# The gated input of a streaming encoder layer, computed with tokens on partitions and turned by VectorE

## The chip, the cores and the metric

The kernel runs on one core of a Trainium2 chip. The metric is the device time of one execution in microseconds (us). The kernel before took 1996.45 us, the median of three runs (1996.19 to 1996.85).

## The reference

One layer of a streaming encoder is computed for 384 tokens: 256 of a new stream and 8 x 16 of running streams. D_MODEL is 2048, D_CONV is 1024, there are 8 heads of 128, and everything is float32. Cut to what matters:

```python
h = rmsnorm(x, norm_mix_g)
proj = h @ w_in            # columns: GLU in (2 x 1024) | q | k | v | forget | gate A | gate B
u = glu_in[..., :D_CONV] * jax.nn.sigmoid(glu_in[..., D_CONV:])
ext = jnp.concatenate([conv_buf, u], axis=1)          # 30 older rows ahead
z = layernorm(causal_dwconv(ext, conv_dw_w, conv_dw_b), conv_ln_g, conv_ln_b)   # 31 taps
a_out = (z * jax.nn.sigmoid(z)) @ conv_pw_out
new_conv = ext[:, -(CONV_W - 1):]                     # an output
b_out = attn_fn(q, k, v, logf) @ w_att_out            # 8 heads, logits + cumsum of log f
x = x + (gate_a * a_out + gate_b * b_out) @ w_out
x = x + (silu(dwconv3(g_half)) * u_half) @ w_down     # up-projected from rmsnorm(x)
```

## The kernel before

Every product runs on TensorE as three matmuls: both operands are split into a high and a low part, and high x high, high x low and low x high are added in PSUM. The loop `gemm` (L227) does a list of jobs, a job being one strip of 512 weight columns over 16 k-steps (8 in some). Two k-steps make a unit: one weight tile `raw` of 128 x 2 x 512 is fetched by SyncE's DMA queue (L139), ScalarE copies its high part (`hi`, L148), VectorE subtracts to get the low part (`lo`, L149). `ahead(3)` asks for up to three units in advance, and `raw`, `hi` and `lo` have three buffers each, so no split can be more than three units ahead of TensorE. PSUM is divided into five `acc` buffers for jobs and three `misc` buffers, most of them for side work.

After each k-step `tick` runs side work: items put off with `after`, then one step of the attention generator, then one step of the convolution generator. TensorE follows the source. On VectorE, ScalarE and SyncE a scheduler sets the order from dependencies and priorities: a split is moved up by SPLIT_AHEAD, attention by ATT_AHEAD, an evacuation of PSUM by EVAC_AHEAD. `queued` chains an instruction behind the last queued one on its engine.

The stages are: the V, Q and K projections; the GLU stage (4 jobs, 64 k-steps) with attention and the start of the convolution as side work; the gates GA and GB (8 jobs) with the rest of the convolution and then its LayerNorm as side work; the output projections; the feed-forward part.

In the GLU stage head h stands at k-step 5 + 6h plus an offset: `head_operands` at +1 (VectorE turns the cached keys, `kTs`, L611, and pads the queries, `qz`), `head_scores` at +4 (TensorE L622 to L630 into three `misc` buffers, VectorE L636 to L640, ScalarE L639 and L641), `head_probs` at +9 (TensorE transposes into two `misc` buffers, which ScalarE's `pT`, L650, and VectorE's `pz`, L653, empty), `head_out` at +12 (`on`, `attT`), `head_last` at +14 (`attT`, L676). Head h+1's scores so stand one k-step behind head h's probabilities.

The weights of GLU job g are 256 columns of each half. The job is of kind "A": the weights are stationary and the result has features on partitions, four blocks of 128 x 384. Evacuation (L702) is four VectorE multiplications by `rs1b` (the norm's factor, spread over partitions by L336 to L344), two sigmoids and two products on GpSimd, into `ut`, features on partitions. All other jobs are of kind "B": tokens on partitions, three blocks of 128 x 512.

The convolution handles the 8 blocks of 128 channels one after another, 17 k-steps apart; block c's tap w (L752 for w = 0, L754 for the rest, 128 x 384 on VectorE) stands at step 17c + w, so in most k-steps two taps stand. Three steps ahead of a block's first tap `fill(c)` builds `ext`: a VectorE transpose of the old state (L731), three ScalarE copies (L733, L736, L737), and for the state that is handed out two TensorE transposes of `ut` (L740, L741), two ScalarE copies and two DMAs.

Of the kernel before, what the change touches and what calls it, by code (L numbers as in the profile page):

```python
# [29 lines left out]
CONV_FIRST, CONV_LAG = 24, 17  # L30
# [3 lines left out]
SPLIT_AHEAD, ATT_AHEAD, EVAC_AHEAD = 150, 250, 400  # L34
# [6 lines left out]
def hybrid_step(  # L41
# [36 lines left out]

    mm = nc.tensor.matmul
    tr = nc.tensor.transpose  # L80
    tt = nc.vector.tensor_tensor
    stt = nc.vector.scalar_tensor_tensor
    ts = nc.vector.tensor_scalar
# [28 lines left out]
    def newton_rsqrt(r, s, m):  # L112
        queued(nc.scalar.activation(s, m, AF.Sqrt), in_first())
        nc.vector.reciprocal(r, s)
        tt(s, r, r, op=ALU.mult)
        tt(s, s, m, op=ALU.mult)
        ts(s, s, -0.5, 1.5, op0=ALU.mult, op1=ALU.add)
        tt(r, r, s, op=ALU.mult)
# [27 lines left out]
    def split_rows(hi, lo, raw, o, k):  # L146
        first = in_first()
        queued(nc.scalar.copy(hi[:, k, :o], raw[:, k, :o]), first)  # L148
        queued(tt(lo[:, k, :o], raw[:, k, :o], f(hi[:, k, :o]), op=ALU.subtract), first)  # L149
# [77 lines left out]
    def gemm(jobs, sides=(), wide=False):  # L227
        for js in jobs:
            js = js if isinstance(js, tuple) else (js,)
            for j in js:  # L230
                nb = 4 if j["kind"] == "A" else NTT
                j["ps"] = [(misc_tile if i == 2 and (wide or j is not js[0]) else acc_tile)() for i in range(nb)]
            for j, k in [(j, k + i) for k in range(0, js[0]["nk"], 2) for j in js for i in range(2)]:
# [7 lines left out]
                for m in range(nb):  # L241
                    s = slice(m * P, (m + 1) * P)
                    if j["kind"] == "A":
                        o = ps[m][:, :NT]
                        mm(o, hi[:, kk, s], ah, start=st, stop=False)  # L245
                        mm(o, hi[:, kk, s], al, start=False, stop=False)  # L246
                        mm(o, lo[:, kk, s], ah, start=False, stop=sp)  # L247
                    else:
                        o = ps[m][:, :n]
                        mm(o, ah[:, s], hi[:, kk, :n], start=st, stop=False)  # L250
                        mm(o, ah[:, s], lo[:, kk, :n], start=False, stop=False)  # L251
                        mm(o, al[:, s], hi[:, kk, :n], start=False, stop=sp)  # L252
                if sp:
                    with tc.high_priority(offset=EVAC_AHEAD):
                        for m in range(nb):
                            j["evac"](m, ps[m])
                    if "post" in j:
# [5 lines left out]
    def blocks(rows, put):  # L263
        src = rows.rearrange("p t (m b j) -> p b m t j", m=4, b=4)
        for b in range(4):
            for a in range(4):
                nc.vector.transpose(put(a, slice(32 * b, 32 * b + 32)), src[32 * a:32 * a + 32, b])  # L267
# [8 lines left out]
    def job(kind, nk, act, evac, n=512, done=None):  # L276
        d = dict(kind=kind, nk=nk, act=act, evac=evac, n=n)
# [12 lines left out]
    def x_chunk(c):  # L290
# [5 lines left out]
        with tc.high_priority(offset=EVAC_AHEAD):  # L296
            queued(nc.scalar.activation(hi, ps[:, :NT], AF.Identity, scale=g))  # L297
# [4 lines left out]
    with tc.manual_schedule(engines={ENG.SP, ENG.Activation, ENG.DVE}):  # L302
        nc.vector.memset(junk[:, 0:1], 0.0)
        nc.scalar.dma_start(gm_row[:], norm_mix_g[0].rearrange("(c p) -> c p", p=P))
        nc.scalar.activation(junk[:, 1:2], junk[:, 0:1], AF.Identity)
# [16 lines left out]
        nc.vector.tensor_copy(gm[:], pv[:, :16])  # L322
# [10 lines left out]
    rs1b = cp.tile([P, NT], F32, name="rs1b")  # L333
# [6 lines left out]
    def over_partitions(dg, dst):  # L340
# [3 lines left out]
        nc.scalar.copy(dst, ps[:, :NT])  # L344
# [46 lines left out]
    def small_columns():  # L391
        ps = misc_tile()
        tr(ps[:, :R_N], vrow[:R_N, :], ident[:R_N, :R_N])
        nc.vector.tensor_copy(col[:], ps[:, :R_N])
        ts(qgs[:], col[:, R_QG:R_QG + 1], float(P) ** -0.5, None, op0=ALU.mult)

    def first_norm():
        for c in range(2, 16, 2):
# [6 lines left out]
            if c % 4 == 2:  # L405
                for t in range(NTT):
                    n = c // 4
                    sq = nc.scalar.activation(junk[:], xs[n][:, t, :], AF.Square, accum_out=ssx[:, t, n:n + 1])
# [9 lines left out]
        with tc.high_priority(offset=EVAC_AHEAD):  # L418
            nc.vector.tensor_reduce(mt[:], ssx[:], axis=mybir.AxisListType.X, op=ALU.add)
            ts(mt[:], mt[:], 1.0 / DM, EPS, op0=ALU.mult, op1=ALU.add)  # L420
            r = rsqrt(mt[:], [P, NTT], p_x0, "r1")
            nc.vector.tensor_copy(rs1[:], r[:])
# [3 lines left out]
        yield  # L426
        dg = diagonals(p_x0.tile([P, NTT, P], F32, name="r1d"), rs1)
        yield
        yield
        over_partitions(dg, rs1b[:])  # L430
# [6 lines left out]
    def tok_job(dst, c0, n, sq):  # L437
        d = job("B", 16, ha, tok_evac(dst, c0, n))

        def post():  # L440
            for t in range(NTT):
                for h in range(c0 // P, (c0 + n) // P):
                    jk = p_qkv.tile([P, P], F32, tag="jk", bufs=2, name="jk")
                    nc.scalar.activation(jk[:], dst[:, t, h * P:(h + 1) * P], AF.Square,
# [4 lines left out]
    def tok_evac(dst, c0, n, shared=True):  # L449
        def ev(t, ps):  # L450
            if shared and t % 2:
                ts(dst[:, t, c0:c0 + n], ps[:, :n], rs1[:, t:t + 1], None, op0=ALU.mult)
            else:
                queued(nc.scalar.activation(dst[:, t, c0:c0 + n], ps[:, :n], AF.Identity, scale=rs1[:, t:t + 1]),
# [4 lines left out]
    v_jobs = [job("B", 16, ha, tok_evac(vt, 344 * i, 344, shared=i == 2), n=344) for i in range(3)]  # L459
# [11 lines left out]
    nc.scalar.activation(e[:], e[:], AF.Exp, scale=-1.0)  # L471
    ts(r[:], e[:], 2.0, None, op0=ALU.add)
    nc.vector.reciprocal(r[:], r[:])
# [27 lines left out]
    def bias_rows():  # L501
        for _ in range(6):
            yield
        for i in range(2):
# [3 lines left out]
            nc.vector.tensor_copy(cw[:, i * 124:(i + 1) * 124], ps[:, :124])  # L508
            nc.vector.tensor_copy(fw[:, i * 66:(i + 1) * 66], ps[:, 128:128 + 66])
# [5 lines left out]
        nc.scalar.activation(crow[:, :2 * P], ps[:H, :2 * P], AF.Copy, scale=-1.0)  # L515
        ps = misc_tile()
        mm(ps[:H, :P], lg[:, 2, :], bm[:], start=True, stop=True)
        nc.scalar.activation(crow[:, 2 * P:], ps[:H, :P], AF.Copy, scale=-1.0)
# [3 lines left out]
        nc.scalar.copy(drow[:], ps[:64, :P])  # L522
# [18 lines left out]
    def q_panel(n):  # L541
        blocks(qt[:, :, 512 * n:512 * (n + 1)], by_feature(attT[:, 4 * n:4 * n + 4]))
        for h in range(4 * n, 4 * n + 4):
            nc.scalar.activation(attT[:, h], attT[:, h], AF.Identity, scale=qgs[:])
# [64 lines left out]
    def head_past_keys(d):  # L609
        kTs = p_att.tile([P, 8, P], F32, tag="kTs", bufs=1, name="kTs")  # L610
        nc.vector.transpose(kTs[:].rearrange("p b k -> p (b k)"), kcs[d["h"]][:])  # L611
        d["kTs"] = kTs

    def head_operands(d):
        head_past_keys(d)
        d["bs"] = bss[d["h"]]
        nc.vector.tensor_copy(qz[d["h"] % 2][:, :, :, 0:16], by_stream(attT[:, d["h"], 2 * P:]))
# [489 lines left out]
```

## Time and profile before

| what | before |
|---|---|
| median of 3 runs | 1996.45 us |
| the profiled execution | 1998.56 us |
| its span, first to last instruction | 1996.7 us |
| granted TensorE clock, mean | 0.999 |
| TensorE busy | 1986.5 us (99%) |
| VectorE busy | 1305.3 us (65%) |
| ScalarE busy | 743.2 us (37%) |
| VectorE busy in 214 to 386 us (GLU stage) | 142.22 of 172 us |
| VectorE busy in 386 to 600 us (gates) | 167.21 of 214 us |

The profiled execution lies 2.11 us over the median, 1.86 us of it outside the span. A matmul of 512 columns takes 0.39 us from start to end, but the next one starts 0.23 us after it, so the rate of TensorE is read from start to start, and so it is with VectorE: of a run of equal instructions the timeline gives start, length and count. "L754" is line 754 of the kernel before.

### The profile page before, as it was taken

To read this page: it belongs to the slowest core of one execution; us is meant where nothing else is said; L and a number is where in the kernel's file an instruction comes from. 1 tells how busy PE (TensorE), PEld (TensorE's weight loads), DVE (VectorE), ACT (ScalarE), POOL (GpSimd) and SP (SyncE) were. 2 spreads that over 40 slices of the span, in tenths; PEclk is the share of its full clock that TensorE was granted. 3 is DMA by queue.
4 is the path that set the end of the run, shared out by engine and by line. 5 is a ranking of instruction groups with operands and counts; after the bars stand their busy time and mean duration, and the time that the engine had idled before them with its cause. 6 is when DMAs were issued, how large, how long until landed. Compare 5 with 4: busy or idle time off the path is not lost.

```text
span 1996.7 us, 24449 instructions
## 1 busy us (share of the span) xinstructions
PE 1986.5 (99%) x9383; PEld 1676.0 (84%) x9383; DVE 1305.3 (65%) x1908; ACT 743.2 (37%) x1077; POOL 89.5 (4%) x216
## 2 busy tenths in 40 slices
PE   9999999999999999999999999999999999999999
PEld 9888999888888888888888888888888888888887
DVE  4455889788755487676867683377673376638663
ACT  5535354433334433344333432233332233323321
POOL 1000011100000000000000000010000000000000
PEclk9999999999999999999999999999999999999999
DMA  6564767444443334534344443444433444343443
GB/s 184 149 188 117 216 154 161 141 140 131 130 129 124 128 125 163 165 122 137 119 137 126 129 134 129 129 126 127 136 129 132 132 118 137 128 133 120 138 158 106
DMA packets 209254, 275.98 MB, mean 138 GB/s; under 512 B 55878, under 2 KB 96729, under 8 KB 209129
## 3 DMA queue, kind: packets, MB, share of 16 engines
q1 hardware_dynamic: 208817, 273.85, 46.0%
q8 instruction: 73, 1.20, 0.3%
q0 software_dynamic: 288, 0.57, 0.1%
q14 instruction: 44, 0.36, 0.1%
q10 hardware_dynamic: 32, 0.01, 0.0%
HBM read 266.98 MB, written 7.86 MB: 138 GB/s over the span
## 4 chain that ended last, share of the span: by engine, by line
PE 96%; DVE 2%; DMA 1%; issue 0%; SPq 0%; ACT 0%; DVEq 0%; ACTq 0%
PE acc L252 20%; PE acc L250 20%; PE acc L251 20%; PE misc L252 10%; PE misc L251 10%; PE misc L250 10%; PE acc L245 2%; PE acc L247 2%; PE acc L246 2%; DVE lo L149 1%; DMA raw<-in_w_in_dram 0%; DVE mixT L267 0%; DVE ut L754 0%; DMA vc<-in_cache_v_dram 0%; DMA bs<-c_dr 0%
## 5 line engine op out<-in xcount | busy, mean ns | idle before, releaser
L149 DVE TENSOR_TENSOR lo<-raw,hi 128x1024 fp32r<-128x1024 f32 (+2 forms) x481 | 580.5, 1207 | 530.7 <-ACT hi L148 526.8
L148 ACT CAST hi<-raw 128x1024 fp32r<-128x1024 f32 (+2 forms) x481 | 496.3, 1032 | 970.1 <-PE misc L252 841.1
L250 PE MATMUL acc<-hi,xg 128*128 128x512 f32 x704 | 274.9, 390 | 0.0
L252 PE MATMUL acc<-hi,xg 128*128 128x512 f32 x704 | 273.9, 389 | 0.0
L251 PE MATMUL acc<-lo,xg 128*128 128x512 f32 x704 | 273.9, 389 | 0.0
L250 PE MATMUL acc<-hi,hT 128*128 128x512 f32 (+1 forms) x512 | 193.0, 377 | 0.5 <-ACT hT L297 0.5
L252 PE MATMUL acc<-hi,hT 128*128 128x512 f32 (+1 forms) x512 | 190.4, 372 | 0.2
L251 PE MATMUL acc<-lo,hT 128*128 128x512 f32 (+1 forms) x512 | 190.3, 372 | 0.0
L250 PEld LDWEIGHTS acc<-hi,xg 128*128 128x128 f32 x704 | 132.1, 188 | 28.4
L754 DVE SCALAR_TENSOR_TENSOR ut<-ext,cw,ut 128x384 f32<-128x384 f32 x240 | 151.9, 633 | 6.0
L252 PEld LDWEIGHTS acc<-hi,xg 128*128 128x128 f32 x704 | 132.1, 188 | 27.5
L251 PEld LDWEIGHTS acc<-lo,xg 128*128 128x128 f32 x704 | 132.2, 188 | 27.1
L252 PE MATMUL misc<-hi,xg 128*128 128x512 f32 x352 | 137.0, 389 | 0.0
L250 PE MATMUL misc<-hi,xg 128*128 128x512 f32 x352 | 137.0, 389 | 0.0
L251 PE MATMUL misc<-lo,xg 128*128 128x512 f32 x352 | 136.9, 389 | 0.0
L250 PE MATMUL acc<-hi,act 128*128 128x512 f32 x352 | 136.9, 389 | 0.0
L251 PE MATMUL acc<-lo,act 128*128 128x512 f32 x352 | 136.9, 389 | 0.0
L252 PE MATMUL acc<-hi,act 128*128 128x512 f32 x352 | 136.9, 389 | 0.0
L267 DVE STREAM_TRANSPOSE extf<-tok 32x384 f32<-32x384 f32 x176 | 100.3, 570 | 30.9 <-ACT tok L988 28.2
L267 DVE STREAM_TRANSPOSE uT<-tok 32x384 f32<-32x384 f32 x176 | 100.3, 570 | 29.7 <-ACT tok L988 26.9
L250 PEld LDWEIGHTS acc<-hi,hT 128*128 128x128 f32 x512 | 96.2, 188 | 16.1 <-ACT hT L297 1.0
L252 PEld LDWEIGHTS acc<-hi,hT 128*128 128x128 f32 x512 | 96.1, 188 | 15.7 <-DVE hT L298 0.7
(325 smaller groups left out, 3133.8 us busy)
## 6 DMA issues: line engine op xcount, KB each, us to landing
raw<-in_w_up_dram SPq DMA_DIRECT2D x176, 512.0 KB
raw<-in_w_in_dram SPq DMA_DIRECT2D x96, 512.0 KB
raw<-in_w_down_dram SPq DMA_DIRECT2D x88, 512.0 KB
raw<-in_w_in_dram SPq DMA_DIRECT2D x64, 256.0 KB
raw<-in_w_out_dram SPq DMA_DIRECT2D x32, 512.0 KB
raw<-in_w_att_out_dram SPq DMA_DIRECT2D x16, 512.0 KB
raw<-in_conv_pw_out_dram SPq DMA_DIRECT2D x16, 512.0 KB
raw<-in_w_in_dram SPq DMA_DIRECT2D x23, 344.0 KB
```

The source lines that it names most:

```text
L148: queued(nc.scalar.copy(hi[:, k, :o], raw[:, k, :o]), first)
L149: queued(tt(lo[:, k, :o], raw[:, k, :o], f(hi[:, k, :o]), op=ALU.subtract), first)
L245: mm(o, hi[:, kk, s], ah, start=st, stop=False)
L246: mm(o, hi[:, kk, s], al, start=False, stop=False)
L247: mm(o, lo[:, kk, s], ah, start=False, stop=sp)
L250: mm(o, ah[:, s], hi[:, kk, :n], start=st, stop=False)
L251: mm(o, ah[:, s], lo[:, kk, :n], start=False, stop=False)
L252: mm(o, al[:, s], hi[:, kk, :n], start=False, stop=sp)
L267: nc.vector.transpose(put(a, slice(32 * b, 32 * b + 32)), src[32 * a:32 * a + 32, b])
L754: stt(o, v, wc, o, op0=ALU.mult, op1=ALU.add)
```

## The change

- The GLU jobs become kind "B", and the kind "A" goes. Block t of a job now holds 128 tokens; columns 0 to 255 are the gate, 256 to 511 the value.
- Evacuation per job: three ScalarE sigmoids (128 x 256, straight from PSUM) and three VectorE `scalar_tensor_tensor` (128 x 256, from PSUM) into `ur`, tokens on partitions. `glu_done` then puts sixteen VectorE transposes of 32 x 192 (`ut<-ur`) into the next four k-steps, four a step. `rs1b` and the six matmul passes that spread it go.
- `fill` loses its two TensorE transposes, two ScalarE copies and two DMAs; the state is handed out by two DMAs from `ur` after the last job.
- A wrapper, `InOrder`, chains every VectorE and ScalarE instruction through the GLU stage in source order, evacuations excepted, which are still moved up. ATT_AHEAD goes. After the stage the scheduler orders again by priority.
- The normalization of a head's probabilities moves to a step of its own (`head_scale`, at +5), with one reciprocal for three. The cached keys are loaded two heads ahead, and the loads of the side work get SPLIT_AHEAD. The convolution starts two k-steps later (CONV_FIRST 24 to 26).

The core of the diff (plain renamings to the wrapped engines and of `job` left out):

```diff
-CONV_FIRST, CONV_LAG = 24, 17
+CONV_FIRST, CONV_LAG = 26, 17
-SPLIT_AHEAD, ATT_AHEAD, EVAC_AHEAD = 150, 250, 400
+SPLIT_AHEAD, EVAC_AHEAD = 150, 400
+    chained = []
+    class InOrder:
+        def __init__(self, eng):
+            self.eng = eng
+        def __getattr__(self, name):
+            op = getattr(self.eng, name)
+            def call(*a, **kw):
+                d = op(*a, **kw)
+                if chained:
+                    queued(d)
+                return d
+            return call
+    dve, act = InOrder(nc.vector), InOrder(nc.scalar)
...
-                    if j["kind"] == "A":
-                        o = ps[m][:, :NT]
-                        mm(o, hi[:, kk, s], ah, start=st, stop=False)
-                        mm(o, hi[:, kk, s], al, start=False, stop=False)
-                        mm(o, lo[:, kk, s], ah, start=False, stop=sp)
-                    else:
-...
+                    o = ps[m][:, :n]
+                    mm(o, ah[:, s], hi[:, kk, :n], start=st, stop=False)
+                    mm(o, ah[:, s], lo[:, kk, :n], start=False, stop=False)
+                    mm(o, al[:, s], hi[:, kk, :n], start=False, stop=sp)
                 if sp:
+                    held, chained[:] = chained[:], []
                     with tc.high_priority(offset=EVAC_AHEAD):
...
+                    chained[:] = held
...
-    def blocks(rows, put):
+    def blocks(rows, put, quarters=range(4)):
-        for b in range(4):
+        for b in quarters:
             for a in range(4):
-                nc.vector.transpose(put(a, slice(32 * b, 32 * b + 32)), src[32 * a:32 * a + 32, b])
+                dve.transpose(put(a, slice(32 * b, 32 * b + 32)), src[32 * a:32 * a + 32, b])
...
-        dg = diagonals(p_x0.tile([P, NTT, P], F32, name="r1d"), rs1)
-        over_partitions(dg, rs1b[:])
...
-            nc.vector.reciprocal(mx[:, i:i + 1], mx[:, 6 + i:7 + i])
-            nc.scalar.activation(v, v, AF.Identity, scale=mx[:, i:i + 1])
+    def head_scale(d):
+        dve.reciprocal(mx[:, 0:3], mx[:, 6:9])
+        for i, (_, o, n) in enumerate(d["segs"]):
+            act.activation(v, v, AF.Identity, scale=mx[:, i:i + 1])
...
-                with tc.high_priority(offset=ATT_AHEAD):
-                    step(d)
-                if step is head_operands and d["h"] + 1 < H:
-                    load_k(d["h"] + 1)
+                step(d)
+                with tc.high_priority(offset=SPLIT_AHEAD):
+                    if step is head_operands and d["h"] + 2 < H:
+                        load_k(d["h"] + 2)
...
     def glu_evac(g):
-        def ev(m, ps):
-            if m < 2:
-                tt(sgb[m][:], ps[:, :NT], rs1b[:], op=ALU.mult)
-                nc.scalar.activation(sgb[m][:], sgb[m][:], AF.Sigmoid)
-            else:
-                tt(u, ps[:, :NT], rs1b[:], op=ALU.mult)
-                nc.gpsimd.tensor_tensor(u, u, sgb[m - 2][:], op=ALU.mult)
+        def ev(t, ps):
+            act.activation(sgb[:], ps[:, 0:256], AF.Sigmoid, scale=rs1[:, t:t + 1])
+            stt(ur[:, t, 256 * g:256 * (g + 1)], ps[:, 256:512], rs1[:, t:t + 1], sgb[:], op0=ALU.mult, op1=ALU.mult)
+    def glu_done(g):
+        def done():
+            for b in range(4):
+                after(b, lambda b=b: blocks(ur[:, :, 256 * g:256 * (g + 1)], by_feature(ut[:, 2 * g:2 * g + 2]), [b]))
+            if g == 3:
+                nc.sync.dma_start(sample_conv[0, :, 14:30, :], ur[:, 2, :])
+                nc.sync.dma_start(prompt_conv[0, 0], ur[98:128, 1, :])
...
-            tr(ps[:, :P], ut[:, c, 2 * P:], ident[:])
-            tr(ps[:32, P:2 * P], ut[:, c, 224:256], ident[:])
-            nc.scalar.copy(su[:, 0, :], ps[:, :P])
-            nc.scalar.copy(su[:32, 1, :], ps[:32, P:2 * P])
-            nc.sync.dma_start(sample_conv[0, :, 14:30, c * P:(c + 1) * P], su[:, 0, :])
-            nc.sync.dma_start(prompt_conv[0, 0, :, c * P:(c + 1) * P], su[2:32, 1, :])
...
+    chained.append(True)
-    gemm([job("A", 16, ha, glu_evac(g)) for g in range(4)], [att_steps, conv_steps])
+    gemm([job(16, ha, glu_evac(g), done=glu_done(g)) for g in range(4)], [att_steps, conv_steps])
     drain(att_steps)
+    chained.clear()
```

What this makes of the order shows at three places on VectorE. The instructions of the changed kernel all carry the wrapper's line, L89, so they are told apart by their tiles. The first place is the end of GLU job 0, where head 0's `pz` (its probabilities, padded) and the evacuation meet. Before:

```order
L149 TENSOR_TENSOR lo<-raw,hi 128x1024 x2
L653 COPY pz_1992<-misc 128x8x16
L706 TENSOR_TENSOR sgb<-acc,rs1b 128x384 x2
L710 TENSOR_TENSOR ut<-acc,rs1b 128x384 x2
L636 ISA pr,mx<-misc,bs 128x128
```

After (`ur` takes the gated product, `ut<-ur` are the turns):

```order
L89 STREAM_TRANSPOSE kTs<-kc 128x1024
L89 COPY qz_1981<-attT 128x8x16
L89 SCALAR_TENSOR_TENSOR ur<-acc,rs_145,sgb 128x256 x3
L89 TENSOR_TENSOR lo<-raw,hi 128x1024
L89 COPY pz_1982<-misc 128x8x16
L89 STREAM_TRANSPOSE ut<-ur 32x6x32 x4
L89 ISA pr,mx<-misc,bs 128x128
```

`pz` stood ahead of the evacuation; now it stands behind it and behind one more split.

The second place is the end of GLU job 2, where taps come two a k-step (`ut<-ext,cw,ut`). Before:

```order
L754 SCALAR_TENSOR_TENSOR ut<-ext,cw,ut 128x384
L706 TENSOR_TENSOR sgb<-acc,rs1b 128x384 x2
L710 TENSOR_TENSOR ut<-acc,rs1b 128x384 x2
L640 RECIPROCAL mx<-mx 128x1
L665 COPY on<-misc 128x128
L754 SCALAR_TENSOR_TENSOR ut<-ext,cw,ut 128x384
L670 COPY attT<-misc 128x256
L754 SCALAR_TENSOR_TENSOR ut<-ext,cw,ut 128x384 x2
L149 TENSOR_TENSOR lo<-raw,hi 128x1024
L754 SCALAR_TENSOR_TENSOR ut<-ext,cw,ut 128x384 x3
L676 COPY attT<-misc 128x128
```

After, from the evacuation to the second `attT`:

```order
L89 SCALAR_TENSOR_TENSOR ur<-acc,rs_145,sgb 128x256 x3
L89 STREAM_TRANSPOSE ut<-ur 32x6x32 x4
L89 COPY on<-misc 128x128
L89 COPY attT<-misc 128x256
L89 SCALAR_TENSOR_TENSOR ut<-ext,cw,ut 128x384 x2
L89 TENSOR_TENSOR lo<-raw,hi 128x1024
L89 STREAM_TRANSPOSE ut<-ur 32x6x32 x4
L89 STREAM_TRANSPOSE kTs<-kc 128x1024
L89 COPY qz_1981<-attT 128x8x16
L89 SCALAR_TENSOR_TENSOR ut<-ext,cw,ut 128x384 x2
L89 STREAM_TRANSPOSE ut<-ur 32x6x32 x4
L89 COPY attT<-misc 128x128
```

Twelve turns, four taps, a split, the keys of the next head and two small copies now stand between the evacuation and the second `attT`; behind it follow two taps, a split and four more turns, and then `pz`. Before, seven taps, a split and two small copies stood there.

The third place is in the gates, from one block's `ext` to past the next block's first taps. Before:

```order
L149 TENSOR_TENSOR lo<-raw,hi 128x1024
L754 SCALAR_TENSOR_TENSOR ut<-ext,cw,ut 128x384 x6
L149 TENSOR_TENSOR lo<-raw,hi 128x1024
L754 SCALAR_TENSOR_TENSOR ut<-ext,cw,ut 128x384 x4
L149 TENSOR_TENSOR lo<-raw,hi 128x1024
L754 SCALAR_TENSOR_TENSOR ut<-ext,cw,ut 128x384 x5
L149 TENSOR_TENSOR lo<-raw,hi 128x1024
L754 SCALAR_TENSOR_TENSOR ut<-ext,cw,ut 128x384 x4
L731 STREAM_TRANSPOSE ext<-sc 128x8x32
L149 TENSOR_TENSOR lo<-raw,hi 128x1024 x3
L752 TENSOR_SCALAR ut<-ext,cw,col 128x384
L754 SCALAR_TENSOR_TENSOR ut<-ext,cw,ut 128x384 x5
```

After:

```order
L89 STREAM_TRANSPOSE ext<-sc 128x8x32
L89 SCALAR_TENSOR_TENSOR ut<-ext,cw,ut 128x384
L89 TENSOR_SCALAR ut<-ext,cw,col 128x384
L89 SCALAR_TENSOR_TENSOR ut<-ext,cw,ut 128x384 x2
L89 TENSOR_TENSOR lo<-raw,hi 128x1024
L89 SCALAR_TENSOR_TENSOR ut<-ext,cw,ut 128x384 x6
L89 TENSOR_TENSOR lo<-raw,hi 128x1024
L89 SCALAR_TENSOR_TENSOR ut<-ext,cw,ut 128x384 x5
L89 TENSOR_TENSOR lo<-raw,hi 128x1024
L89 SCALAR_TENSOR_TENSOR ut<-ext,cw,ut 128x384 x6
L89 TENSOR_TENSOR lo<-raw,hi 128x1024
```

Before, three splits in a row follow the state's transpose, with no tap between; now taps go on, and five or six stand in front of every split. Over the whole stretch from the first turns after the last GLU job on, 36 splits stand beside 179 taps and 5 first taps; before, the 43 splits of the like stretch stood beside 158 and 5.

177 lines of the change are left out of this document (86 added, 91 removed).

## The prediction

> **What bounds the kernel now.** I read the page first, then TensorE's waits, then the timeline around the only long wait.
>
> ```profile
> span 1996.7 us, 24449 instructions
> PE 1986.5 (99%) x9383; PEld 1676.0 (84%) x9383; DVE 1305.3 (65%) x1908; ACT 743.2 (37%) x1077; POOL 89.5 (4%) x216
> PE 96%; DVE 2%; DMA 1%; issue 0%; SPq 0%; ACT 0%; DVEq 0%; ACTq 0%
> PE misc L630 <- DVE kTs L611: 2.5, 1, 2.5
> ```
>
> TensorE is busy 99% of the span and is 96% of the chain that ends last. So only two things move the time: matmuls that go, and waits that TensorE gets or loses. VectorE's 65% is an average, and the change works in the stages where it is higher:
>
> ```profile
> 300.00:340.00 40.00, 40.00 (x316) 37.78 (x315) 35.66 (x88) 20.04 (x42) 4.13 (x6) 1.00 0.72 170
> 340.00:350.00 10.00, 10.00 (x63) 9.93 (x64) 9.43 (x17) 4.11 (x7) 2.90 (x3) 1.00 0.67 130
> 400.00:430.00 30.00, 30.00 (x135) 24.77 (x134) 27.89 (x42) 10.51 (x15) 1.11 (x3) 1.00 0.47 130
> ```
>
> In these windows (length, then busy TensorE, weight loads, VectorE, ScalarE, GpSimd, then the clock) VectorE is busy 35.66 of 40, 9.43 of 10 and 27.89 of 30 us while TensorE never waits. There is little room there for more.
>
> The one long wait costs twice:
>
> ```profile
> 353.23 0.64 PE L630 MATMUL misc<-kTs,qz 128*32 128x128 f32 x16 [2.50 <-DVE kTs L611]
> 354.46 0.52 PE L245 MATMUL acc<-hT,hi 128*128 128x384 f32 x1
> 357.34 0.52 PE L245 MATMUL acc<-hT,hi 128*128 128x384 f32 x1
> ```
>
> After 2.50 us of waiting, the ten matmuls from 354.46 to 357.34 start 0.32 us apart ((357.34 - 354.46) / 9), where the rows below give 0.173: about 1.6 us more with the two half-slowed ones beside them. I count such a dip with each wait of 2.5 us or more and with none below.
>
> The Trainium skill (TensorE: Matmul & The Clock Gate, section "HAM oscillation — how this bites in real kernels") states that idle gaps over some 3.4 us are what costs the clock. By that rule a wait of 2.5 us costs only itself and 1.6 us falls from the sum below; here the 2.50 us wait was followed by half pace, so the trace does not agree.
>
> **What goes.** The rate of both forms:
>
> ```profile
> 216.19 0.33 PE L245 MATMUL acc<-hT,hi 128*128 128x384 f32 x1
> 220.35 0.33 PE L245 MATMUL acc<-hT,hi 128*128 128x384 f32 x1
> 409.65 0.39 PE L250 MATMUL acc<-hi,hT 128*128 128x512 f32 x1
> 412.82 0.39 PE L252 MATMUL acc<-hi,hT 128*128 128x512 f32 x1
> 437.98 0.39 PE L252 MATMUL misc<-hi,hT 128*128 128x512 f32 x1
> 438.21 0.27 PE L740 MATMUL misc<-ident,ut 128*128 128x128 f32 x1
> 438.67 0.40 PE L251 MATMUL acc<-lo,hT 128*128 128x512 f32 x1
> 85.74 0.83 PE L343 MATMUL misc<-r1d,ones 128*128 128x128 f32 x6
> 86.64 0.40 PE L251 MATMUL acc<-lo,hT 128*128 128x512 f32 x1
> ```
>
> 24 matmuls of 384 columns take 4.16 us (0.173 each), 14 of 512 take 3.17 us (0.2264). The GLU stage has 64 x 12 = 768 of the first and gets 64 x 9 = 576 of the second: 133.1 against 130.4, **-2.7 us**. From 438.21 to 438.67 there are the two transposes and one matmul; less the matmul's 0.23 that is 0.23 a block, and eight blocks give **-1.9**. The spread of `rs1b` takes 0.90 from 85.74 to 86.64 with one matmul in it: **-0.7**. The long wait came from keys turned late; these are now fetched two heads ahead and are moved up at SyncE's queue, so I let the 2.5 and its 1.6 go: **-4.1**. Together **-9.4 us**.
>
> **What comes on VectorE.** A turn of 32 x 192 and a product of 128 x 256 from PSUM are not in the trace. The nearest rows (count, busy us, mean ns, idle before):
>
> ```profile
> L267 DVE STREAM_TRANSPOSE qt<-kt 32x384 f32<-32x384 f32 x27 | 15.4, 570 | 0.4
> L731 DVE STREAM_TRANSPOSE ext<-sc 128x256 f32<-128x256 f32 x8 | 3.5, 440 | 1.6 <-DMA sc<-in_state_conv_dram 1.4
> L611 DVE STREAM_TRANSPOSE kTs<-kc 128x1024 f32<-128x1024 f32 x7 | 8.7, 1238 | 0.0
> L710 DVE TENSOR_TENSOR ut<-acc,rs1b 128x384 f32<-128x384 f32 x8 | 4.2, 554 | 0.0
> L670 DVE COPY attT<-misc 128x256 f32<-128x256 f32 x8 | 3.3, 419 | 0.5 <-PE misc L669 0.5
> L640 DVE RECIPROCAL mx<-mx 128x1 f32<-128x1 f32 x24 | 3.5, 150 | 2.5 <-ACT pr L639 2.5
> ```
>
> Between 440 ns for 256 columns and 1238 for 1024 lie 1.04 ns a column over 174 fixed; 384 columns give 573 (570 stands), so 192 give 0.37 us. I take 0.38; the ends are half of 570 (0.29) and 570 itself. A product I take at 0.40, beside the copy's 0.419. Per job: 16 x 0.38 + 3 x 0.40 = 7.3 us in four k-steps, where four multiplications took 2.2. The stage's total says little: 64 turns add 24 us, and 31 taps (20 us at 0.655) leave the stage by the order. The places do.
>
> The Trainium skill (VectorE: DVE Perf Modes, section "Two Vector instructions with no wait between them") states that an instruction whose start quadrant differs from the one before starts only when all earlier ones are done. The sixteen turns change quadrants; by that rule each costs its full duration, estimated as the 0.37 above, and the sum stays within 0.1 us a job of what it is.
>
> **First places: ends of jobs 0 and 1.** Head 1's scores follow the last matmul of job 0 at once and need the two `misc` buffers that `pT` and `pz` of head 0 empty.
>
> ```profile
> L148 ACT CAST hi<-raw 128x1024 fp32r<-128x1024 f32 x99 | 103.7, 1047 | 187.8 <-PE misc L252 123.0 <-PE acc L246 45.4 <-issue 8.6
> L650 ACT COPY pT<-misc 128x512 f32<-128x512 f32 x8 | 4.7, 588 | 13.9 <-PE misc L649 13.9
> 408.89 1.22 DVE L149 TENSOR_TENSOR lo<-raw,hi 128x1024 fp32r<-128x1024 f32 x1
> 410.03 3.23 DVE L754 SCALAR_TENSOR_TENSOR ut<-ext,cw,ut 128x384 f32<-128x384 f32 x5
> 413.18 1.22 DVE L149 TENSOR_TENSOR lo<-raw,hi 128x1024 fp32r<-128x1024 f32 x1
> ```
>
> Behind the last block come its sigmoid and product (0.5 to 0.6 us), then `hi` 1.05, `lo` 1.14 (410.03 - 408.89), `pz` 0.2: 2.9 us after the last matmul, of which the first scores cover 0.4: **+2.5, and a dip of 1.6**. At the end of job 1, head 3's `pz` has eight turns (3.0 us) more in front, partly covered by the k-step before head 4's scores: **+1.8**. Head 0's first keys stand behind all turns of the last k panel: **+0.4**. These three are zero if VectorE is early enough, and 1.5 more in all if a turn takes 0.57.
>
> **Second place: end of job 2.** Here two taps stand in each step. A run of n taps takes 0.535 + 0.655 (n - 1): five take 3.15 (413.18 - 410.03). From the evacuation to head 6's `pz` VectorE has, by the order, 3 products 1.2, 16 turns 6.1, eight taps in four pairs 4.8, two splits 2.3, the keys 1.2, small copies 1.1: 16.6 us. TensorE needs it four k-steps on, 4 x 2.04 = 8.2 (9 x 0.2264 each) plus 1.4 of attention matmuls. The first products start 1.1 us before the job's end. 16.6 - 9.6 - 1.1 = **+5.9, and a dip of 1.6**. Ends: 4.5 with turns of 0.29, 8.9 with 0.57.
>
> **Third place: the gates.** There a unit lasts TensorE 18 x 0.2264 = 4.08 us. From the first turns behind the last job the order has 179 taps in 45 runs, 36 splits, 12 turns, 8 attention splits, 5 first taps and 5 state transposes until split 36 of this stretch:
>
> ```profile
> 393.81 1.48 DVE L795 TENSOR_TENSOR aHL<-attT,aHL 128x384 fp32r<-128x384 f32 x3
> 395.22 0.60 DVE L754 SCALAR_TENSOR_TENSOR ut<-ext,cw,ut 128x384 f32<-128x384 f32 x1
> 402.46 0.45 DVE L731 STREAM_TRANSPOSE ext<-sc 128x256 f32<-128x256 f32 x1
> 405.23 0.47 DVE L752 TENSOR_SCALAR ut<-ext,cw,col 128x384 f32<-128x384 f32 x1
> 405.74 3.23 DVE L754 SCALAR_TENSOR_TENSOR ut<-ext,cw,ut 128x384 f32<-128x384 f32 x5
> ```
>
> 134 x 0.655 + 45 x 0.535 + 36 x 1.14 + 12 x 0.38 + 8 x 0.47 + 5 x 0.51 + 5 x 0.4 = 165.8 us (0.47 is 1.41 / 3, 0.51 is 405.74 - 405.23). TensorE would do these 36 units in 146.9. VectorE's lead is at most 6.0 us: `hi` and `lo` have three buffers, so a split can begin two units ahead of its use (8.2), less 1.05 and 1.14. 165.8 - 146.9 - 6.0 = **+12.9 us**, in waits of half a microsecond a unit, too short for a dip by the above. Before, 43 splits stood beside 158 taps: 154 us of VectorE in 175 of TensorE. What held the taps back there:
>
> ```profile
> DVE lo L149 <- ACT hi L148: 38.1, 17, 3.4
> DVE ut L752 <- PE misc L741: 4.0, 2, 2.0
> ```
>
> Between 395 and 600 us the splits themselves waited 38.1 us for ScalarE's `hi`, which waits for TensorE to free a buffer: VectorE was early. The first tap waits behind `fill`'s transposes on TensorE; these go, and the scheduler packs the taps closer. Ends: with a tap at its busy 0.633 the term is 10; with a lead of 3 us, 16.
>
> The rest is off the path: 16 fewer reciprocals (0.15 each) and ScalarE's fewer copies cover nothing that TensorE waits for; GpSimd loses eight products; two DMAs in place of 16 land behind the stage, on a queue whose transfers the three `raw` buffers cover, and cost 1 us or so if one of them is late.
>
> **The sum**, against the profiled 1998.56: -9.4 + 0.4 + 2.5 + 1.6 + 1.8 + 5.9 + 1.6 + 12.9 = +17.3, so 2015.9, and 2013.8 at the median, which lies 2.11 lower. Forecast: **2014 us**. Within 0.2% (1992.5 to 2000.4) is about what a measurement here cannot tell from no change. With all costs at their low ends (turns 0.29, no dips, no waits at jobs 0 and 1): 1987.1 + 4.5 + 10 = 2002. At the high ends: 2013.8 + 3.0 + 1.5 + 3.1 + 2.3 (twelve turns in the gates) + 2.3 for two more dips = 2026.
>
> **Rivals.**
> - Faster: the leads hold. Split buffers are three units deep and 31 taps leave the GLU stage, so VectorE could meet each end of a job with a full lead, and in the gates it could win back lead wherever fewer than five taps stand in front of a split. Then only the -9.4 is left: 1987. For it: the splits' 38.1 us of waiting above. Against it: `ur` cannot start before the job's last matmuls, whatever the lead, and no instruction passes another on VectorE. It decides where the order's VectorE time per unit is 4.08 us or less; by the rows it is 4.6. Chance 0.2.
> - Waits in the GLU stage alone (the gates keep up): 1987.1 + 13.8 = 2000.9. Against it is the count of taps. Chance 0.13.
> - Late splits in the gates alone: 1987.1 + 12.9 = 2000.0. For it: VectorE is relieved of taps before the end of job 2, and the pairs may come early. Chance 0.13.
> - The change does less than it says: if evacuations and turns cost what they save, 1996; inside the two above.
>
> **How the numbers follow.** Both together, my forecast, 0.54; its own range is 2002 to 2026. The two cases around 2000 lie half within 0.2%, half above. Faster 0.2, same 0.13, slower 0.67. A range from 1990 to 2026 leaves out most of the faster case (0.13) and little above.
>
> **What would show it.** On TensorE's waits: `misc` L622 to L630's successors waiting for `pT` or `pz` at the ends of jobs 0 to 2 (2.5, 1.8, 5.9 us), and half pace behind the first and third. In the gates: matmuls that read `lo` waiting for VectorE half a microsecond a unit, with VectorE busy all of 400 to 530 us. Wrong it is if the splits there still wait for `hi`, if a turn takes under 0.3 us, or if TensorE's waits in the GLU stage stay below 3 us in all.

## The result and the profile after

The changed kernel takes 2019.3 us, the median of four runs (2017.78 to 2020.1), against 1996.48 of the kernel before: a ratio of 1.0111 (95% interval 1.0096 to 1.0126). Forecast were 2014 us, between 1990 and 2026. The profiled execution took 2019.11 us; its span was 2017.2 us, 20.5 more than the 1996.7 of the kernel before.

The page of the changed kernel: its span, its engines, its chain.

```profile
span 2017.2 us, 24004 instructions
PE 1991.3 (99%) x9169; PEld 1652.7 (82%) x9169; DVE 1313.9 (65%) x1949; ACT 739.1 (37%) x1063; POOL 81.0 (4%) x208
PE 86%; DVE 10%; issue 2%; ACT 1%; DMA 1%; SPq 0%; DVEq 0%; ACTq 0%
```

VectorE has grown from 2% to 10% of the chain that ends last. What TensorE waits for between 200 and 700 us (us in total, times, longest):

```profile
PE misc L630 <- ACT pT L89: 8.9, 2, 4.8
PE misc L632 <- DVE pz L89: 5.4, 2, 3.5
PE misc L630 <- DVE attT L89: 1.6, 1, 1.6
PE misc L636 <- DVE qz L89: 0.8, 1, 0.8
PE acc L261 <- DVE lo L89: 0.7, 2, 0.4
PE misc L354 <- DVE ln L89: 0.2, 1, 0.2
```

16.7 us of waits belong to the scores of the heads in the GLU stage, 0.7 to late splits in the gates. The windows of the GLU stage and of the convolution's part of the gates (length, busy TensorE, weight loads, VectorE, ScalarE, GpSimd, then the clock, the share of the DMA engines and GB/s):

```profile
213.00:405.00 192.00, 175.24 (x998) 140.45 (x997) 138.61 (x303) 79.17 (x143) 8.97 (x17) 0.94 0.58 149
405.00:600.00 195.00, 194.29 (x856) 160.18 (x856) 175.30 (x273) 68.03 (x87) 12.88 (x17) 1.00 0.47 135
```

TensorE idles 16.76 us in the first and 0.71 in the second, and the mean clock of the first is 0.94. The half-pace stretches are longer than I had allowed. After the 3.50 us wait at 371.99:

```profile
374.32 0.63 PE L261 MATMUL acc<-lo,hT 128*128 128x512 f32 x1
378.16 0.49 PE L261 MATMUL acc<-lo,hT 128*128 128x512 f32 x1
```

From the one to the other it is nine starts on, 0.427 us apart, where 0.226 is full pace. Four such stretches hold 25 matmuls at 0.43, 5 us over full pace, and the attention matmuls and half-slowed ones beside them lose as well.

From the last V job's evacuation to the first sigmoid of the second gate job, the changed kernel takes 20.5 us more (212.74 to 468.95 against 213.89 to 449.57). Idle accounts for 16.8 - 2.5 = 14.3, the new form for -2.7, the five pairs of fill's transposes that the stretch held before for -1.2; by difference the slow clock takes some 10 us more than before.

Nor did all waits come at the ends of jobs. The scores of head 1 (4.80 us, at 254.46, the end of job 0) and of head 3 (4.13, at 293.75, inside job 1) waited for `pT`. For the first of them ScalarE shows why:

```profile
252.88 1.04 ACT L89 CAST hi<-raw 128x1024 fp32r<-128x1024 f32 x1 [2.93 <-DMA raw<-in_w_in_dram]
253.83 0.58 ACT L89 COPY pT<-misc 128x512 f32<-128x512 f32 x1
```

The split in front of `pT` stood 2.93 us for a weight tile. What SyncE sent before it:

```profile
240.03 0.61 SPq L606 DMA_DIRECT2D bs<-d_dr  x1
245.91 2.37 SPq L593 DMA_DIRECT2D kc<-in_cache_k_dram  x4
248.38 7.71 SPq L156 DMA_DIRECT2D raw<-in_w_in_dram  x8
```

From 234 to 248 us no weight tile went out; then eight pieces did, two to a tile. At head 3 the keys stood even between the two pieces of a tile; its split began at 292.17:

```profile
277.15 0.41 SPq L156 DMA_DIRECT2D raw<-in_w_in_dram  x1
285.74 2.34 SPq L593 DMA_DIRECT2D kc<-in_cache_k_dram  x4
288.13 0.80 SPq L156 DMA_DIRECT2D raw<-in_w_in_dram  x1
```

Before the change, at the time of the first wait, tiles went out whole, with one or two pieces of keys between:

```profile
242.97 0.40 SPq L587 DMA_DIRECT2D kc<-in_cache_k_dram  x1
245.34 0.90 SPq L139 DMA_DIRECT2D raw<-in_w_in_dram  x2
246.29 0.46 SPq L587 DMA_DIRECT2D kc<-in_cache_k_dram  x1
248.31 0.88 SPq L139 DMA_DIRECT2D raw<-in_w_in_dram  x2
```

### The profile page after: what moved, and what is told of

It reads as the page before. It is cut to its first block, busy times and chain, and to the rows that moved or that the text cites. A ratio compares the mean times of both kernels' runs of the same rounds, so it can differ in the third digit from the quotient of the medians.

```text
span 2017.2 us, 24004 instructions
## 1 busy us (share of the span) xinstructions
PE 1991.3 (99%) x9169; PEld 1652.7 (82%) x9169; DVE 1313.9 (65%) x1949; ACT 739.1 (37%) x1063; POOL 81.0 (4%) x208
## 4 chain that ended last, share of the span: by engine, by line
PE 86%; DVE 10%; issue 2%; ACT 1%; DMA 1%; SPq 0%; DVEq 0%; ACTq 0%
PE acc L260 19%; PE acc L262 19%; PE acc L261 19%; PE misc L260 9%; PE misc L262 9%; PE misc L261 9%; DVE ut L89 5%; DVE lo L89 3%; DVE qt L89 1%; DMA raw<-in_w_in_dram 1%; ACT hi L89 0%; DVE mixT L89 0%; DVE sgA L89 0%; PE misc L636 0%; DVE kt L89 0%
## 5 line engine op out<-in xcount | busy, mean ns | idle before, releaser
L89 DVE TENSOR_TENSOR lo<-raw,hi 128x1024 fp32r<-128x1024 f32 (+2 forms) x481 | 580.0, 1206 | 549.1 <-ACT hi L89 545.2
L89 ACT CAST hi<-raw 128x1024 fp32r<-128x1024 f32 (+2 forms) x481 | 495.8, 1031 | 956.3 <-PE misc L262 836.6
L260 PE MATMUL acc<-hi,hT 128*128 128x512 f32 (+1 forms) x704 | 273.1, 388 | 0.8 <-ACT hT L89 0.8
L261 PE MATMUL acc<-lo,hT 128*128 128x512 f32 (+1 forms) x704 | 267.9, 381 | 0.7 <-DVE lo L89 0.7
L262 PE MATMUL acc<-hi,hT 128*128 128x512 f32 (+1 forms) x704 | 267.8, 380 | 0.2
L260 PEld LDWEIGHTS acc<-hi,hT 128*128 128x128 f32 x704 | 133.9, 190 | 26.0 <-issue 2.3
L262 PEld LDWEIGHTS acc<-hi,hT 128*128 128x128 f32 x704 | 133.7, 190 | 24.2 <-DVE hT L89 0.7
L261 PEld LDWEIGHTS acc<-lo,hT 128*128 128x128 f32 x704 | 133.9, 190 | 23.6 <-DVE lo L89 1.6
L89 DVE SCALAR_TENSOR_TENSOR ut<-ext,cw,ut 128x384 f32<-128x384 f32 x240 | 139.0, 626 | 0.9
L89 DVE STREAM_TRANSPOSE extf<-tok 32x384 f32<-32x384 f32 x176 | 100.3, 570 | 30.9 <-ACT tok L89 28.2
```

The lines of the kernel that those rows point to most:

```text
L89: d = op(*a, **kw)
```

## The experiments

Ratios are to the kernel before on the same chip, whose median there was 1997.6 to 1998.5 us. Three theories stood: **order** (the fixed order puts `pT` and `pz` behind splits, evacuations and turns), **fetch** (the raised side loads make weight tiles late) and **load** (VectorE has too much work with the turns).

**1. Probabilities one k-step earlier**

```diff
-(5, head_scale), (9, head_probs),
+(5, head_scale), (8, head_probs),
```

> Head probabilities one k-step earlier (offset 9 to 8), so that pT and pz come ahead of the next split in the fixed order; all else as in the changed kernel (2019.3 us). Order theory (pT and pz wait because a split, whose weight tile has not landed, stands ahead of them on ScalarE and VectorE): the waits of 4.80 and 4.13 us of the scores for pT go, with their two half-pace stretches of about 2.2 and 3.1 us, and the wait of 3.5 for pz at the end of job 2 loses the four turns and the split, about 2.6: 2019.3 - 4.8 - 4.1 - 5.3 - 2.6 = 2002 to 2005 us. Load theory (VectorE simply has too much work in this stage because of the 64 turns): the waits move to another instruction and the time stays over 2014. Fetch theory (late weight tiles): the wait goes over to the matmuls that use the tile, over 2012.

Measured: 2011.1 us, 1.0066 (1.0051 to 1.0081). This kernel leaves out `head_last` of the first seven heads, whose place in the table of steps it takes, and with it seven transposes and copies. The waits for `pT` are gone, but new ones of 1.8 to 2.4 us stand at other steps, 14.5 us in all up to 700 us. The waits moved on from the order of `pT` alone, so the order is not the only cause. As those steps are missing too, the run settles no more.

**2. No fixed order**

```diff
-    chained.append(True)
-                step(d)
+                with tc.high_priority(offset=ATT_AHEAD):
+                    step(d)
```

> The changed kernel without the fixed order: VectorE and ScalarE go by the scheduler's priorities in the GLU stage, attention moved up by 250 as before. Order theory: all of the 16.8 us of waits and most of the half-pace stretches go: 1988 to 1996 us. Load theory: the ends of jobs 1 and 2 keep waits of 4 us or more: 2003 us or more. My gate term's heir (VectorE late in the gates): if taps are again made back to back on one block, the matmuls wait for lo in the gates, up to 10 us.

Measured: 2015.0 us, 1.0087 (1.0072 to 1.0102). The order theory alone falls: the waits did not go, they changed their name.

```profile
PE acc L261 <- DVE lo L89: 14.9, 6, 4.8
PE acc L260 <- ACT hi L89: 2.5, 2, 1.8
```

Now TensorE waits for the splits themselves. The wait of 3.87 us that ends at 277.02 is for this split:

```profile
259.81 1.11 SPq L156 DMA_DIRECT2D raw<-in_w_in_dram  x2
271.57 1.98 ACT L89 CAST hi<-raw 128x1024 fp32r<-128x1024 f32 x2
273.50 2.33 DVE L89 SCALAR_TENSOR_TENSOR ut<-ext,cw,ut 128x384 f32<-128x384 f32 x3
275.76 1.21 DVE L89 TENSOR_TENSOR lo<-raw,hi 128x1024 fp32r<-128x1024 f32 x1
```

Its tile had been asked for at 259.81 and was there when `hi` began, straight behind other work of ScalarE; TensorE read that `hi` at 272.65. What `lo` stood behind from then on were taps on VectorE. Six and five taps stand right ahead of `lo` in the two other waits of more than 3 us (at 300.01 and 324.56). So these waits come from the order that the scheduler chose and not from a late tile. Still the raised loads have a part in it: experiment 6 differs from this one by the loads alone and has none of these waits. How the loads change the scheduler's order is not shown.

**3. The fixed order alone, in the kernel before**

```diff
+    chained.append(True)
     gemm([job("A", 16, ha, glu_evac(g)) for g in range(4)], [att_steps, conv_steps])
     drain(att_steps)
+    chained.clear()
```

(with the wrapper and the release around evacuations, as in the change)

> The kernel before with the fixed order alone (all VectorE and ScalarE instructions of the GLU stage in source order, evacuations still moved up; features on partitions, no turns). Order theory: pT and pz stand behind a split here too, so scores wait for them at head 1 and the following heads: 8 us or more over before, 2004 to 2012 us. Load theory: without turns no wait: 1993 to 1998 us.

Measured: 2004.4 us, 1.0031 (1.0020 to 1.0043), six waits of 0.3 to 1.7 us. The fixed order costs some 6 us without any turn and without the new loads: the order theory's part.

**4. Keys asked for four k-steps later**

```diff
-                    if step is head_operands and d["h"] + 2 < H:
+                    if step is head_scale and d["h"] + 2 < H:
                         load_k(d["h"] + 2)
```

> The cached keys of the head after next are asked for four k-steps later, so SyncE does not stand waiting for their buffer ahead of a weight tile; all else as changed. Fetch theory (SyncE's queue makes the weight tile late, and this is what pT waits for): the waits of 4.80 and 4.13 us shrink to about 2 each, one half-pace stretch goes: 2011 to 2014 us. Order theory alone: the split still stands ahead of pT and pz, at most 2 us less: 2017 to 2020.

Measured: 2010.4 us, 1.0065 (1.0050 to 1.0080), 9 us less than the change by the ratios. The wait of 4.80 fell to 1.44 and that of 4.13 is gone, which is the way the fetch theory has it and further than it said; the half-pace stretches behind both went too, so the gain was larger than expected.

**5. All side loads as before the change, the fixed order kept**

```diff
-                with tc.high_priority(offset=SPLIT_AHEAD):
-                    if step is head_operands and d["h"] + 2 < H:
-                        load_k(d["h"] + 2)
+                if step is head_operands and d["h"] + 1 < H:
+                    load_k(d["h"] + 1)
...
-                    with tc.high_priority(offset=SPLIT_AHEAD):
-                        load_state(c)
+                    load_state(c)
-    load_k(1)
```

> The changed kernel with the loads of the side work as before the change: keys one head ahead, no raised priority for keys, values, biases and states; fixed order and turns stay. Fetch theory (SyncE sends the side loads in groups ahead of the weight tiles, and a late tile reaches pT and pz through the fixed order): like the late key load, which won 9 us, or more, since biases, values and states also come out of the way: 2004 to 2010 us; waits for pT under 1 us; the waits for pz behind the turns at the ends of jobs 1 and 2 (1.9, 1.6, 3.5) stay. Order theory without the fetch: 2015 or more, since the keys' buffers and the split's place do not change.

Measured: 2003.9 us, 1.0030 (1.0020 to 1.0040). No wait for `pT` is left:

```profile
PE misc L632 <- DVE pz L89: 6.2, 3, 3.5
PE misc L630 <- DVE attT L89: 1.6, 1, 1.6
```

The loads' order and priority thus cost (1.0111 - 1.0030) x 1996.5 = 16 us, the largest part of the loss. What remains stands at the ends of jobs 1 and 2. At the end of job 0 there is no wait at all: `pT` starts at 246.81 and `pz` at 246.92, ahead of the job's products at 249.22. The fixed order and the turns are the same as in the change, so neither of them alone makes that wait.

**6. Loads as before, no fixed order** (experiments 2 and 5 together)

> The same loads as before the change and no fixed order; the new form of the product and the 64 turns stay. If late weight tiles and the order of pz and pT are all that costs, both are gone here: 1986 to 1993 us, faster than before. If VectorE's turns cost by their length alone: waits for lo or pz of 3 us or more at the ends of jobs, 1998 us or more.

Measured: 1999.8 us, 1.0013 (1.0003 to 1.0022). Not faster; the time fits the second case, but the waits are others: 1.8 us for `kTs` and 5.4 for a head's scores, which must leave `misc`, from 339.26 to 344.69. VectorE in that time:

```profile
340.38 1.23 DVE L89 TENSOR_TENSOR lo<-raw,hi 128x1024 fp32r<-128x1024 f32 x1 [0.76 <-ACT hi L89]
341.52 0.48 DVE L89 SCALAR_TENSOR_TENSOR ur<-acc,rs,sgb 128x256 f32<-128x256 f32 x1
342.03 2.27 DVE L89 STREAM_TRANSPOSE ut<-ur 32x192 f32<-32x192 f32 x6
344.33 0.29 DVE L89 CUSTOM_DVE_ANT_0 pr<-misc,bs 128x128 f32<-128x128 f32 x1
```

The scheduler too puts turns, six of them, ahead of what TensorE waits for. They take 2.3 of the 5.4 us; a split that waited 0.76 us for ScalarE and the job's last product behind it take most of the rest.

**7. The state's transposes back on TensorE**

```diff
+            ps = misc_tile()
+            tr(ps[:, :P], ut[:, c, 2 * P:], ident[:])
+            tr(ps[:32, P:2 * P], ut[:, c, 224:256], ident[:])
...
```

(the two DMAs from `ur` go in return)

> The changed kernel with fill's two TensorE transposes, two ScalarE copies and two DMAs a block put back. Alternation theory (in the changed kernel the taps of two blocks alternate and start 0.53 us apart, because ext of the next block no longer waits for TensorE; a tap right behind one of the same block starts 0.655 after it): the gates have one block at a time again, runs of taps start 0.65 apart, VectorE waits again for the transposes, and the time grows by TensorE's 1.9 us and up to 3 more: 2019 to 2024 us. If the start distance comes from elsewhere, taps stay at 0.53 apart.

Measured: 2018.9 us, 1.0099 (1.0082 to 1.0116). Of 131 pairs of successive taps from 405 to 580 us, 57 start 0.53 us apart and 72 0.655; in the changed kernel it is 125 and 12 of 141, before the change none and all 115. From 500 us on, runs of one block are back. First this kernel, then the changed one:

```profile
511.54 2.57 DVE L89 SCALAR_TENSOR_TENSOR ut<-ext,cw,ut 128x384 f32<-128x384 f32 x4
515.16 3.23 DVE L89 SCALAR_TENSOR_TENSOR ut<-ext,cw,ut 128x384 f32<-128x384 f32 x5
```

```profile
443.70 2.20 DVE L89 SCALAR_TENSOR_TENSOR ut<-ext,cw,ut 128x384 f32<-128x384 f32 x4
451.27 2.73 DVE L89 SCALAR_TENSOR_TENSOR ut<-ext,cw,ut 128x384 f32<-128x384 f32 x5
```

Five taps take 3.23 us on one block and 2.73 where two blocks alternate. The late waits for `lo` in the gates are gone. The time hardly moved, where growth of 1.9 us or more was expected; the waits in the GLU stage changed places as well, so the price of the transposes cannot be read from it.

**8. Loads as before, probabilities earlier, turns in successive k-steps**

```diff
-(5, head_scale), (9, head_probs), (12, head_out), (14, head_last)
+(5, head_scale), (8, head_probs), (12, head_out), (15, head_last)
```

> As the combined kernel (fixed order, loads as before, probabilities at offset 8, last step at 15), but with the sixteen turns in four successive k-steps as in the change. It tells what the spreading of the turns is worth. If the turns in front of pz and attT at the ends of jobs 1 and 2 are the rest of the cost: waits of 1 to 4 us more than the combined kernel and one half-pace stretch more, 1998 to 2002 us. If the order of pz alone mattered: as the combined kernel, within 1 us of 0.9991 of before.

Measured: 2002.5 us, 1.0023 (1.0014 to 1.0032), just above the range. Waits of 1.9, 1.55 and 3.5 us stand behind the turns as in experiment 5, now for `attT` more than for `pz`: the earlier probabilities alone gave next to nothing.

**9. The same with the turns in every second k-step**

```diff
-                after(b, lambda b=b: blocks(ur[:, :, 256 * g:256 * (g + 1)], ...
+                after(2 * b, lambda b=b: blocks(ur[:, :, 256 * g:256 * (g + 1)], ...
```

> Fixed order kept, loads as before the change, head probabilities one k-step earlier (offset 8) with the last step of a head at 15, and the turns in every second k-step in place of every one. Order and fetch theories: no weight tile is late, pT and pz stand ahead of the split, and eight of the sixteen turns stand between the end of a job and the next pz: waits of under 3 us in all and one half-pace stretch at most: 1988 to 1996 us. Load theory: no better than the loads alone, 2004 or more.

Measured: 1996.2 us, 0.9991 (0.9982 to 1.0001), at the upper end of the range and not clear of the kernel before. One wait of 1.8 us for `attT` is left at the end of job 2, with its half-pace stretch. Against experiment 8 only the turns moved: 0.0032 of the time, 6.4 us.

**10. Taps ordered by block**

```diff
+                    held_taps.append((c, w))
+            if t < 64 - CONV_FIRST or t % 4 == 3 or ...:
+                flush()        # sorted by block; chained tap to tap after the GLU stage
```

> The changed kernel with the taps of the gates ordered by block, up to four of one block in a row, and kept in that order among themselves. Alternation theory: three of four successive taps start 0.655 us apart, with no other change to them; the scheduler places fewer of them in front of a split (five for six), so the time stays within 4 us of the changed kernel's. If another cause had shortened the start distance (fewer ScalarE or TensorE accesses, the missing transposes), it stays at 0.53.

Measured, in one execution: 2020.6 us. Of 136 pairs 98 start 0.655 us apart and 33 0.53. The transposes are still gone here, so it is the order of the blocks that sets the distance. In the gates TensorE now waits 1.7 us for `lo`, against 0.7 in the changed kernel.

**11. The last step back at 14, turns of jobs 1 and 2 four k-steps later**

```diff
-                              (12, head_out), (15, head_last)):
+                              (12, head_out), (14, head_last)):
...
+                after(2 * b + (4 if g in (1, 2) else 0), lambda b=b: blocks(ur...
```

> The combined kernel with the last step of a head back at 14, in the same k-step as the next head's probabilities and ahead of them, and the turns of jobs 1 and 2 put off by four k-steps, past the scores that waited. If the last waits (1.8 us for attT at the end of job 2, with its half-pace stretch of about 2) come from turns ahead of attT: they go, and 3 to 4 us with them: 0.997 to 0.998 of before (1991 to 1993 us where before is 1997). If they come from the last step's place, right ahead of the scores: the same, but a wait shows at another head if the turns matter there.

Measured: 1998.0 us, 0.9999 (0.9989 to 1.0008). The wait for `attT` is gone, and one of 3.2 us has come for `on`, which `head_last` transposes: two k-steps after `head_out` it stood behind a split that waited for ScalarE.

**12. Experiment 9 with the turns of jobs 1 and 2 four k-steps later**

```diff
-                after(2 * b, lambda b=b: ...
+                after(2 * b + (4 if g in (1, 2) else 0), lambda b=b: ...
```

> The combined kernel (last step of a head at 15) with the turns of jobs 1 and 2 four k-steps later, past the scores that waited 1.82 us for attT. If those turns are what attT stood behind: the wait and its half-pace stretch go, 0.997 to 0.998 of before. If a wait on a split or on another step takes its place, as with the last step at 14: 0.999 to 1.000 of before.

Measured: 1991.6 us, 0.9970 (0.9958 to 0.9982), faster than both kernels. Its span, and what TensorE waits for between 200 and 700 us:

```profile
span 1990.0 us, 24003 instructions
PE misc L636 <- DVE qz L89: 0.8, 1, 0.8
PE misc L354 <- DVE ln L89: 0.2, 1, 0.2
```

No half-pace stretch is left in the GLU stage. The first four gains of the prediction, 9.4 us, would make 1987.3 of the span of 1996.7; 1990.0 is what came.

## Why the prediction was right, and where not

The direction was right, and so were the mechanism and the size of the waits at the ends of jobs 1 and 2. That the total of 2014 came so near 2019 is luck: the gates, the largest term of the sum (+12.9), cost 0.7, while the waits for `pT` came out 6.4 us longer than the sum has them and the slow clock about 8 us.

- **What goes**, -9.4. Experiment 12 comes within 2.7 us of it; the four gains were tested together, not one by one. The reason for the last one does not hold: experiments 5, 8, 9 and 12 ask for keys one head ahead, as before the change, and have no wait for `kTs` either. It is back, at 1.8 us, in experiment 6, which has the same loads and no fixed order. So the moved loads, the costliest part of the change, were not needed for what they were to win.
- **Price of a turn.** Forecast 0.38 us from the line through two other transposes; the row of the changed kernel says 370 ns for one, and the timeline gives four in 1.51 to 1.53, so each starts when the one before has ended. Sixteen at 0.37 for 0.38 are 0.16 us a job, a little more than the 0.1 in the prediction. Products took 0.48 for the 0.40 assumed.

```profile
L89 DVE STREAM_TRANSPOSE ut<-ur 32x192 f32<-32x192 f32 x64 | 23.7, 370 | 1.1
L89 DVE SCALAR_TENSOR_TENSOR ur<-acc,rs,sgb 128x256 f32<-128x256 f32 x12 | 5.6, 481 | 4.4 <-ACT sgb L89 4.4
```

- **Ends of jobs 1 and 2**, +1.8 and +5.9: 1.91 at 315.59, and 1.60 + 3.50 = 5.1 from 367.80 to 371.99. Experiments 8, 9 and 12 confirm that turns ahead of `pz` and `attT` make them. One count was wrong: between the evacuation of job 2 and `pz` the order has six taps in three pairs, not eight in four (and before the change it has six taps up to the second `attT`, not seven). With six the term is 4.7, nearer still to the 5.1. VectorE's timeline shows the second, from the job's last products to `pz`:

```profile
357.05 0.48 DVE L89 SCALAR_TENSOR_TENSOR ur<-acc,rs,sgb 128x256 f32<-128x256 f32 x1 [0.47 <-ACT sgb L89]
365.90 1.52 DVE L89 STREAM_TRANSPOSE ut<-ur 32x192 f32<-32x192 f32 x4
367.45 0.29 DVE L89 COPY attT<-misc 128x128 f32<-128x128 f32 x1
370.09 1.53 DVE L89 STREAM_TRANSPOSE ut<-ur 32x192 f32<-32x192 f32 x4
371.65 0.29 DVE L89 COPY pz<-misc 128x128 f32<-128x128 f32 x1
```

- **End of job 0**, +2.5 and a dip: 4.80 came, and 4.13 at head 3, where I forecast nothing. (Head 0's first keys, +0.4, cost 0.8.) Where the products and a split stand ahead of `pT` and `pz` and the tile comes in time, as in experiment 4, the term is 1.44 + 0.39 = 1.8 us and no dip; in the changed kernel a late weight tile holds `hi` for 2.93 us more, and in experiment 5, where `pz` comes ahead of the products, there is no wait. The step that failed is the sentence that lets the keys be "fetched two heads ahead and are moved up at SyncE's queue" and counts only the gain. I saw that a moved load must be followed past its queue, and did not do it for the weight tiles behind it: `kc` has two buffers, so the load of head h + 2 waits until head h is turned, and SyncE's queue stands still with the weight tiles behind it. Experiment 4 shows 9 us for the time at which the keys are asked for, experiment 5 shows 16 for all the moved loads. In the fixed order the late tile reaches TensorE through `pT`. Without the fixed order the moved loads cost about as much (1.0087 in experiment 2, 1.0013 in 6), but there TensorE's long waits are for splits behind taps, by a way that is not shown.
- **Half pace**, +1.6 twice, against 1.6 before: by difference some 10 us more than before came. There were four stretches, not two, each of two to nine slow matmuls that lose 0.20 us apiece instead of the 0.15 of the narrower form; and the attention matmuls before them run slow as well (the pair of L632 takes 0.80 us at 371.99, 0.38 at 234.52).
- **The gates**, +12.9: 0.7 us of waits came. The order was read rightly (five and six taps in front of a split, VectorE idle for 0.2 us between 430 and 540), but the price of a tap was not. I took 0.655 us from runs that all stood on one block, where each tap waits for the one in front of it. Without fill's transposes two blocks are at hand, their taps alternate, and they start 0.53 us apart. With that the sum for the same rows is 179 x 0.53 + 36 x 1.14 + 12 x 0.38 + 8 x 0.47 + 5 x 0.39 + 5 x 0.36 = 148.0 us, for TensorE's 146.9: the lead covers it.

The forecast's case (waits in both stages) therefore did not happen as described; of the rivals, "waits in the GLU stage alone" did, at 2019 in place of 2000.9. The faster rival named the right condition, VectorE's time per unit in the gates at 4.08 us or less; 148.0 / 36 = 4.11 comes so near that the lead carries the rest. Its claim that the leads cover the ends of jobs did not hold.

What stays open: which part of the 20 us of the change each of its remaining edits (one reciprocal for three, CONV_FIRST) carries, how raised loads lead the scheduler to put taps ahead of splits (experiment 2), and how far experiment 1's waits come from the steps that it leaves out.

## What to carry to other kernels

A load moved up in a queue moves everything behind it down: where its buffer is not free yet, the queue stands, and the stream that feeds the bottleneck stands with it. When an order is fixed by hand, look for what the bottleneck waits for next and keep bulk work (turns here, 6 us a job) a few steps behind it; with the loads put back, spreading and delaying the same 64 turns turned a loss of 0.2% into a gain of 0.3%. And take an instruction's price from a row whose neighbours depend on it as they will after the change.

## What the runs showed of the hardware

- A VectorE `scalar_tensor_tensor` of 128 x 384 starts 0.53 us after its forerunner where two blocks alternate (125 pairs in the changed kernel), but 0.65 after one whose result it adds to (all 115 pairs in the kernel before): 0.12 us for a dependency on the instruction right in front. Experiment 10, which put three of four pairs on one block, has 98 pairs of the second kind and 33 of the first.
- Half pace followed a wait of 1.91 us (at 315.59 in the changed kernel) and did not follow one of 1.90 (at 302.01 in experiment 8), nor one of 2.40 (at 293.76 in experiment 1). So a limit on the length of a single wait, such as the 2.5 us that I used, does not tell when the clock drops. The Trainium skill (TensorE: Matmul & The Clock Gate, section "What's actually happening") describes a free-running window; with one, the same wait can fall either way, which agrees with these three, though no run here shows the window itself.
- The slow stretches are alike at both widths, near half speed: 0.32 us a start for 384 columns (0.173 at full pace), 0.427 for 512 (0.226).
